# Output projection with two pairs by seven products, and the ConvFFN's first tiles reordered with six weights' low parts by accumulating transfers

## The chip, the cores and the metric

The kernel runs on one core of a Trainium2 chip. The metric is the device time of one execution in microseconds. The core has a matrix engine (PE, with weight loads shown as PEld), a vector engine (DVE), a scalar engine (ACT), a general engine (POOL) and a queue engine (SP) that issues transfers; each runs its own list of instructions in order and waits on the others through semaphores. Transfers are issued by SP, POOL and ACT, and carried out by 16 DMA engines.

## The reference

One layer of a decoder with 512 prompt tokens and 8 × 8 sample tokens, 576 columns in all, in float32, model width 1024, ConvFFN width 2816:

```python
h = _rmsnorm(x, norm1_g) * (1.0 + sc1) + sh1
...                                   # short convolution branch -> ya, attention branch -> o
yb = o @ w_attn_out
mixed = jax.nn.sigmoid(ga) * ya + jax.nn.sigmoid(gb) * yb
x = x + g1 * (mixed @ w_mix_out)

h2 = _rmsnorm(x, norm2_g) * (1.0 + sc2) + sh2
a, val = jnp.split(h2 @ w_up, 2, axis=-1)
ac, new_ffn = _causal_conv(a, ffn_buf, ffn_conv_w)
x = x + g2 * ((jax.nn.gelu(ac, approximate=False) * val) @ w_down)
```

`sh1, sc1, g1, sh2, sc2, g2` come from `silu(c) @ w_ada + b_ada`, for 9 conditioning rows (one prompt, eight samples).

## The kernel before

**Numbers in two parts.** Everything is held transposed: a tile is 128 channels by 576 tokens. Each float32 operand of a matmul is split into a high part (ACT copies it into the type float32r) and a low part (DVE subtracts the high part from the value). A product of one 128-wide output takes the 8 blocks of 128 input channels in turn (`kstep`), each as three passes, high × high, high weight × low operand, low weight × high operand, and each pass as two matmuls of 256 and 320 columns: 48 matmuls (`product`). `product_g` does one of the two column groups alone.

**Weights.** `load_w` issues a 512 KB load of 1024 × 128 weights from SP into one of four `raw` buffers; `split_w` makes `whi` (ACT) and `wlo` (DVE), each with five buffers, `split_w_slots` makes them in halves of 512 (`wh`, `wl`) in the common pool of 57 slots. A `raw` buffer comes free when its last reader is done.

**Pairs by seven products.** In other stages of the kernel two outputs are made together by a Strassen-like scheme with 7 block products instead of 8. `PairOperands` prepares the two channel blocks kp and kp + 4 of the operand: four sums of 288 columns each (DVE), high parts `th`, `nh` (ACT), low parts `tl`, `nl` (DVE), and the block called n3. `pair_weights` prepares the sums of two raw weights in steps named sums1, sums2 (DVE additions), ah, bh, ch, dh (ACT) and al, bl, cl, dl (DVE). `pair_product` then runs parts 1 to 7 of 12 matmuls with 288 columns each and combines the banks of PSUM between them: after part 1 and 3 ACT copies a bank (`p`), after part 2 and 6 DVE subtracts (`uv`), after 4, 6 and 7 the outputs are handed out (out_a0, then out_b0 and out_b1, then out_a1). A dictionary of steps says what other work is issued behind each part.

**Order around the change.** PE, ACT and DVE are pinned to the order of the program text through most of the kernel (`pinned`, class `InOrder`); elsewhere a planner that simulates a timeline orders each engine's list. The stages in question, with the times of the profile of before:

- About 473.5 to 535, the attention output (`w_attn_out`): eight whole products m = 0 to 7. DVE multiplies each result by the gate (`sg<-mm,sg`) and adds `ya`, then the sum is split into `mxh`, `mxl` (`mixed`). A generator (`filler`) puts matmuls of the second modulation block (`side_by_side`, 128 x 512, loaded as `ada` tiles of 256 KB from SP) and the transposes of its rows between the k steps, 11 steps of it to 60 ticks. The pinning ends at m = 3.
- To 588, the output projection (`w_mix_out`): first the 22 small transposes of the ConvFFN state (`state_in`), then five whole products m = 0 to 4, then the outputs 5 to 7 by halves (`mix_late`), first group 0 of all three, then group 1. After each, `residual` updates x (DVE, `x<-mm,modT,x`), ACT squares it and DVE adds the squares into `acc`. The x before the layer comes back from DRAM in two 1152 KB loads on POOL's queue (`x1`).
- Within the group 1 halves: `norm2_rows(0)` sums the squares on PE after k = `NORM2[0]` of output 5, DVE and POOL (a power of −0.5) make the row factors, and `spread_group` spreads them on PE after k = `NORM2[1]` of output 6.
- To 608.4, the first tiles of the ConvFFN: weights a0, v0 and a1 (`ws`; gate columns 0, value columns 0, gate columns 1) side by side, one k step each, while DVE, ACT and POOL make the normalised operand `h2`.
- To 640, the products v1, a2, v2, a3, v3, one after the other. A gate tile goes through pads (ACT), three taps (ACT, then DVE twice), gelu (ACT); then `value` multiplies it with its value product (`cy`, DVE) and ACT and DVE split the result (`fh`, `fl`). Between these the `PairOperands` of `h2` and the weights of the first pair are made.
- From 640 on, `FfnPair` 4 and later, by seven products each.

Of the kernel before, what the change touches and what calls it, by code (L numbers as in the profile page):

```python
# [69 lines left out]
def step_kernel(ctx: ExitStack, tc: tile.TileContext, ins: dict, outs: list):  # L70
# [30 lines left out]
    class InOrder:  # L101


        def __init__(self, engine):
            self.engine = engine
# [5 lines left out]

            return call

    pe, act, dve, pool = (InOrder(e) for e in (nc.tensor, nc.scalar, nc.vector, nc.gpsimd))
    pinned += [pe, act, dve, pool]
    matmul, transpose = pe.matmul, pe.transpose

# [27 lines left out]
    def load_w(src, nk):  # L145

        raw = wp.tile([P, nk, P], F32, tag="raw", name=nm("raw"), bufs=W_BUFS)
        nc.sync.dma_start(raw, src)
        return raw

    def split_w(raw):
        nk = raw.shape[1]
        hi = wp.tile([P, nk, P], F32R, tag="whi", name=nm("whi"), bufs=S_BUFS)
        lo = wp.tile([P, nk, P], F32R, tag="wlo", name=nm("wlo"), bufs=S_BUFS)
        split(hi, lo, raw)
        return (lambda k: hi[:, k, :]), (lambda k: lo[:, k, :])

    def split_w_slots(raw):

# [43 lines left out]
    def halves(ps):  # L203
        return ps[:, 256:512], ps[:, 512:832]

    def product(w, xs):
        ps = mmps()
        for k in range(len(xs)):
            kstep(halves(ps), w, xs, k)
            tick()  # L210
        return pf(ps)
# [17 lines left out]
    class PairOperands:  # L229

        def __init__(self, x, kp, made, values=None):
            self.x, self.kp = (x[kp], x[kp + 4]), kp
            self.r = values and (values[kp], values[kp + 4])
            self.made = made

        def sums(self):
            if not self.r:
# [11 lines left out]
        def high(self):  # L251
            made, (h0, l0), (h1, l1) = self.made, *self.x
            self.th, self.tl = slot("th", F32R), slot("tl", F32R)
            act.activation(self.th, self.t, AF.Copy)
            if self.kp % 2 == 0:
                made["n4"] = slot("nh", F32R), slot("nl", F32R)
            a, b = slice(0, HT), slice(HT, NT)
            at = (a, b)[self.kp % 2]
            nh, nl = made["n4"]
            self.nh, self.nl = nh[:, at], nl[:, at]  # L260
            act.activation(self.nh, self.r[0][:, a], AF.Copy)
            for name, hi, lo, c in (
                ("x00", h0, l0, a), ("n3", h0, l0, b), ("x10", h1, l1, a), ("x11", h1, l1, b),
                ("n1", self.th, self.tl, a), ("t2", self.th, self.tl, b), ("n4", nh, nl, at),
            ):
                made.setdefault("op", {}).setdefault(name, []).append((hi[:, c], lo[:, c]))

        def low(self):
            for lo, src, hi in ((self.tl, self.t, self.th), (self.nl, self.r[0][:, :HT], self.nh)):
                dve.tensor_tensor(out=lo, in0=src, in1=hi.bitcast(F32), op=ALU.subtract)  # L270

        def n3(self):

            (hi, lo), b = self.x[0], slice(HT, NT)
            split(hi[:, b], lo[:, b], self.r[0][:, b])

        def all(self):
            self.sums()
# [105 lines left out]
    def load(dst, src):  # L384
        return tc.keep_in_program_order(nc.sync.dma_start(dst, src))  # L385
# [315 lines left out]
    def state_load(src, n):  # L701
        parts = []
        for m0 in range(0, n, 4):
            c = min(4, n - m0)
            s = slot("st", shape=[P, 512])
            load(s[:16, : c * P], src.rearrange("o b r c -> (o b r) c")[:, m0 * P : (m0 + c) * P])
            parts.append(s)
        return parts

# [413 lines left out]
    def modulation(c0):  # L1123
# [4 lines left out]
        def rows(k):  # L1128
            cols[k] = [slot("ada", shape=[P, 512]) for _ in range(4)]
            for j, t in enumerate(cols[k]):  # L1130
                c = c0 + 512 * j
                nc.sync.dma_start(t, ins["w_ada"][0, k * P : k * P + P, c : c + 512])

        rows(0)
        yield False
# [140 lines left out]
    for n in range(len(gate_cols)):  # L1276
# [6 lines left out]
                steps[7] = lambda m=2 * n - 7: gated(m)  # L1283
        else:
            w_next[0] = weights(kpm(wao, 0), NK)
            raw = load_w(kpm(wao, P), NK)
# [40 lines left out]

    def squares(xt, m, c0=0, c1=NT):
        if m == 0:
            nc.scalar.activation(acc[:, c0:c1], xt[:, c0:c1], AF.Square)  # L1330
        else:
            sq = slot("sq")
            nc.scalar.activation(sq[:, c0:c1], xt[:, c0:c1], AF.Square)
            nc.vector.tensor_tensor(
                out=acc[:, c0:c1], in0=acc[:, c0:c1], in1=sq[:, c0:c1], op=ALU.add
            )

    stF = state_in(state_load(ins["state_ffn_conv"], NF), "stF", NF)
    A2 = cp.tile([P, NK, 9], F32, tag="A2", name="A2")
    affine(A2, 32, 56, NK)  # L1340
    x1t = [wp.tile([P, 4, NT], F32, tag="oh", name=nm("x1"), bufs=2) for _ in range(2)]
    for x in range(2):
        nc.gpsimd.dma_start(x1t[x], xT_dram[x])
    x1 = [x1t[k // 4][:, k % 4, :] for k in range(NK)]
    late = []
    for m in range(NK - 3):
        w = weights(kpm(ins["w_mix_out"][0], m * P), NK)
        if m >= NK - 6:
            late.append(split_w_slots(load_w(kpm(ins["w_mix_out"][0], (m + 3) * P), NK)))
        residual(product(w, mixed), x1[m], 16 + m)  # L1350
        squares(x1[m], m)

    def mix_late(m, g, between=None):
        ps = product_g(late[m - NK + 3], mixed, g, between=between)
        residual(ps, x1[m], 16 + m, *GRP[g])
        squares(x1[m], m, *GRP[g])

# [51 lines left out]

    for m in range(NK - 3, NK):  # L1410
        mix_late(m, 0)
    pinned.append(pe)
    mix_late(NK - 3, 1, (NORM2[0], lambda: norm2_rows(0)))
    R = {}
    ahead = []
# [8 lines left out]
    mix_late(NK - 2, 1, (NORM2[1], first_parts))  # L1424
    mix_late(NK - 1, 1)


    w_up, w_dn = ins["w_up"][0], ins["w_down"][0]

    def ffn_conv(ps, m):  # L1430
        u = padded()
# [154 lines left out]
        return load_w(kpm(w_dn, m * P, m0, m1 - m0), m1 - m0)  # L1586


    ws = [weights(kpm(w_up, c * P), NK) for c in (0, NF, 1)]
    acc2 = [mmps() for _ in range(2)]  # L1590
    first = [halves(x) for x in acc2] + [None]
    pend = [(0, k) for k in range(NK)] + [(1, k) for k in (0, 4, 1, 5, 2, 6, 3, 7)]
    for at, (g, k) in enumerate(pend):
# [12 lines left out]
            norm2_rows(1)  # L1606
        if at == NORM2[4]:
            R[1] = spread_group(r2, 1)
            pinned.extend([dve, act])
        if at == NK:  # L1610
            w_v1 = split_w_slots(load_w(kpm(w_up, FF + P), NK))
        if at == NK + 4:
# [9 lines left out]
    def w_split(raw):  # L1622
        hi, lo = (wp.tile([P, NK, P], F32R, tag=t, name=nm(t), bufs=S_BUFS) for t in ("whi", "wlo"))
        act.activation(hi, raw, AF.Copy)
        low = lambda: dve.tensor_tensor(out=lo, in0=raw, in1=hi.bitcast(F32), op=ALU.subtract)
        return ((lambda k: hi[:, k, :]), (lambda k: lo[:, k, :])), low

    def start(t, ps):
        t.copies(ps)
        t.first_tap()  # L1630
# [15 lines left out]
    tiles[0].low()  # L1646
    tiles[1].taps()
    for g, k in pend[-1 - NORM2[2] :]:
        norm2_whole(g, k)
    ops[0].high()  # L1650
    tiles[1].gelu()
    w_a3, low = w_split(raw[1])
    raw = load_w(kpm(w_up, FF + 3 * P), NK)
    pair = FfnPair(4)
    ops[0].low()
    ops[1].sums()
    value(tiles[1], v1)
    low()
    ops[1].high()
    a2 = product(w_a2, h2)  # L1660
    tiles[1].low()
    ops[1].low()
    ops[2].sums()
    v2 = product(w_v2, h2)
    start(tiles[2], a2)
    ops[2].high()
    tiles[2].taps()
    w_v3, low = w_split(raw)
    tiles[2].gelu()
    low()  # L1670
    ops[2].low()
    steps = pair.prepare()
    nxt = FfnPair(5)
    ops[3].sums()
    ops[3].high()
    steps["ah"]()
    a3 = product(w_a3, h2)
    value(tiles[2], v2)
    tiles[2].low()
    ops[3].low()  # L1680
    steps["sums1"]()
    steps["al"]()
    steps["dh"]()
    steps["bh"]()
    steps["dl"]()
    v3 = product(w_v3, h2)
    start(tiles[3], a3)
    steps["sums2"]()
    tiles[3].taps()
    tiles[3].gelu()  # L1690
    steps["ch"]()
    steps["bl"]()
    steps["cl"]()
    value(tiles[3], v3)
    tiles[3].low()

# [158 lines left out]
```

## Time and profile before

| | us |
|---|---|
| median of 3 runs | 1000.4 |
| lowest and highest run | 1000.04, 1001.07 |
| profiled execution | 1001.41 |
| its span | 999.6 |
| PE busy | 983.2 (98%) |
| DVE busy | 670.7 (67%) |
| ACT busy | 450.8 (45%) |
| POOL busy | 100.3 (10%) |

The profile is one execution with every instruction's start and duration. A line of the table by groups gives the source line, engine, operation, output<-inputs, shapes and count, then busy time and mean ns of one, then idle time before it and what ended that. A timeline row gives start and duration in us. Nearly every instruction has line 109, that of the helper `InOrder`, so groups are told apart by tile names. In the table by stretches each engine's busy time is followed by its count of instructions, then the granted clock of PE, the share of the 16 DMA engines and GB/s. Matmuls overlap in the pipeline: a duration of 0.30 us stands for a step of about 0.13 us to the next.

### The profile page before, as it was taken

How to read it: one execution, taken by the hardware profiler on the slowest of the kernel's cores; microseconds unless marked ns; L12 is line 12 of the kernel's file. 1: busy time of each engine (PE TensorE's matmuls, PEld its weight loads, DVE VectorE, ACT ScalarE, POOL GpSimd, SP SyncE). 2: the span in 40 equal slices, each digit the busy share in tenths (PEclk: the TensorE clock that was granted, in tenths of full speed). 3: DMA queues.
4: the chain of work that ended last, by engine and by line, in shares of the span. 5: the costliest groups of instructions: out<-in, count | busy, mean ns of one | idle time of the engine just before them, and what ended most of it. 6: DMA issues, size and time to landing. Idle time of an engine off the chain costs nothing.

```text
span 999.6 us, 18691 instructions
## 1 busy us (share of the span) xinstructions
PE 983.2 (98%) x7516; PEld 941.8 (94%) x7516; DVE 670.7 (67%) x1241; ACT 450.8 (45%) x835; POOL 100.3 (10%) x271
## 2 busy tenths in 40 slices
PE   7999999999999999999999999999999999999997
PEld 5899999999999989999889999999999999999997
DVE  5736676676463348788454568896569995579953
ACT  5454555545334225545232347554225552235453
POOL 2221101020000000000000021011001110001120
PEclk9999999999999999999999999999999999999999
DMA  9984332233421752235972302223233222323302
GB/s 290 319 253 109 86 90 70 86 116 115 141 76 53 246 180 85 86 106 157 338 231 72 106 11 75 65 85 106 85 101 90 85 85 86 106 65 101 110 10 95
DMA packets 173481, 119.18 MB, mean 119 GB/s; under 512 B 6887, under 2 KB 160846, under 8 KB 173106
## 3 DMA queue, kind: packets, MB, share of 16 engines
q1 hardware_dynamic: 169954, 107.00, 35.3%
q0 software_dynamic: 3296, 10.73, 3.5%
q8 instruction: 59, 0.97, 0.4%
q14 instruction: 28, 0.23, 0.1%
q10 hardware_dynamic: 144, 0.26, 0.1%
HBM read 109.17 MB, written 7.35 MB: 117 GB/s over the span
## 4 chain that ended last, share of the span: by engine, by line
PE 82%; DVE 10%; issue 2%; DMA 2%; ACT 2%; SPq 0%; POOL 0%; POOLq 0%; DVEq 0%; ACTq 0%
PE mm L109 60%; PE aux L109 19%; DVE wlo L109 3%; PE aux L1116 2%; DMA ad<-in_w_ada 2%; PE aux L1016 2%; DVE raw L109 1%; DVE uv L109 1%; DVE y L109 1%; DVE cy L109 1%; DMA raw<-in_w_in 1%; DVE fl L109 1%; SPq L385 0%; DVE wl L109 0%; ACT whi L109 0%
## 5 line engine op out<-in xcount | busy, mean ns | idle before, releaser
L109 ACT ACTIVATE whi<-raw 128x1024 fp32r<-128x1024 f32 (+2 forms) x164 | 168.1, 1034 | 178.6 <-PE mm L109 95.5
L109 DVE TENSOR_TENSOR wlo<-raw,whi 128x1024 fp32r<-128x1024 f32 (+2 forms) x164 | 195.1, 1194 | 48.6 <-ACT whi L109 47.9
L109 PE MATMUL mm<-hh,whi 128*128 128x256 f32 (+2 forms) x560 | 124.6, 299 | 0.6 <-ACT hh L109 0.6
L109 PE MATMUL mm<-hh,wlo 128*128 128x256 f32 (+2 forms) x560 | 121.8, 294 | 0.0
L109 PE MATMUL mm<-hl,whi 128*128 128x256 f32 (+2 forms) x560 | 121.0, 295 | 0.1
L109 PEld LDWEIGHTS mm<-hh,whi 128*128 128x128 f32 x560 | 93.0, 188 | 2.9 <-ACT hh L109 1.2
L109 PEld LDWEIGHTS mm<-hh,wlo 128*128 128x128 f32 x560 | 94.2, 188 | 0.0
L109 PEld LDWEIGHTS mm<-hl,whi 128*128 128x128 f32 x560 | 93.6, 188 | 0.5 <-DVE hl L109 0.5
L109 DVE SCALAR_TENSOR_TENSOR x<-mm,modT,x 128x512 f32<-128x512 f32 (+1 forms) x33 | 22.6, 686 | 71.1 <-PE mm L109 71.0
L109 PE MATMUL mm<-fh,whi 128*128 128x256 f32 (+1 forms) x304 | 65.0, 296 | 0.3 <-DVE rt L109 0.3
L109 PE MATMUL mm<-fl,whi 128*128 128x256 f32 (+1 forms) x304 | 65.1, 295 | 0.0
L109 PE MATMUL mm<-fh,wlo 128*128 128x256 f32 (+1 forms) x304 | 64.9, 295 | 0.0
L109 PE MATMUL mm<-th,whi 128*128 128x288 f32 x208 | 61.7, 297 | 0.7 <-DVE uv L109 0.7
L109 PE MATMUL mm<-th,wlo 128*128 128x288 f32 x208 | 61.6, 296 | 0.6 <-DVE wlo L109 0.6
L109 PE MATMUL mm<-tl,whi 128*128 128x288 f32 x208 | 61.4, 295 | 0.0
L109 PEld LDWEIGHTS mm<-fh,whi 128*128 128x128 f32 x304 | 50.7, 188 | 0.5 <-PE mm L109 0.5
L109 PEld LDWEIGHTS mm<-fl,whi 128*128 128x128 f32 x304 | 51.0, 188 | 0.0
L109 PEld LDWEIGHTS mm<-fh,wlo 128*128 128x128 f32 x304 | 50.8, 188 | 0.0
L867 ACT ACTIVATE s<-s,nmx 128x256 f32<-128x256 f32 (+1 forms) x72 | 34.0, 474 | 32.0 <-DVE nmx L864 31.2
L109 PE MATMUL aux<-2h,whi 128*128 128x288 f32 (+2 forms) x160 | 47.2, 295 | 0.8 <-ACT p L109 0.8
L109 PE MATMUL aux<-2h,wlo 128*128 128x288 f32 (+2 forms) x160 | 47.3, 296 | 0.0
L109 PE MATMUL aux<-2l,whi 128*128 128x288 f32 (+2 forms) x160 | 47.0, 294 | 0.0
(310 smaller groups left out, 2568.8 us busy)
## 6 DMA issues: line engine op xcount, KB each, us to landing
raw<-in_w_in SPq DMA_DIRECT2D x52, 512.0 KB, 4.2
raw<-in_w_up SPq DMA_DIRECT2D x44, 512.0 KB, 3.9
ada<-in_w_ada SPq DMA_DIRECT2D x64, 256.0 KB, 6.0
ad<-in_w_ada SPq DMA_DIRECT2D x32, 256.0 KB, 6.3
raw<-in_w_down SPq DMA_DIRECT2D x16, 512.0 KB, 3.5
raw<-in_w_conv_out SPq DMA_DIRECT2D x8, 512.0 KB, 3.5
raw<-in_w_attn_out SPq DMA_DIRECT2D x8, 512.0 KB, 4.2
raw<-in_w_mix_out SPq DMA_DIRECT2D x8, 512.0 KB, 6.1
```

The lines of the kernel that those rows point to most:

```text
L109: done = getattr(self.engine, name)(*args, **kwargs)
L867: nc.scalar.activation(s[x // 2][:, x % 2, :w], s[x // 2][:, x % 2, :w], AF.Exp, bias=nmx[:, x : x + 1], accum_out=den[:, x : x + 1],)
L1016: done = nc.tensor.matmul(O[HALF[par], :256], vt(i - nkt + 1 + kt)[:, hd * 64 : hd * 64 + 64], pts[kt][:, par * 256 : par * 256 + 256], st ...
L1116: done = nc.tensor.matmul(ps[32 * j : 32 * j + 32, :], cT[:, k, :], cols[k][j], start=(k == 1), stop=(k == NK - 2),)
```

## The change

- **Two pairs in the output projection.** `w_mix_out`'s outputs 1 and 2, and 3 and 4, are made by `pair_product`; output 0 and the halves of 5 to 7 stay. The operands of the pairs are made between the attention output products, whose order becomes 0, 4, 1, 5, 2, 6, 3, 7 so that blocks kp and kp + 4 are there together; the weights of the first pair are prepared there as well (`PAIR_LOW`, `PAIR_HIGH`). `PairOperands` gets a form (`beside`) that keeps the n3 block apart, since the unchanged block of `mixed` is still needed by the later products.
- **Loads and order there.** The attention output weights are loaded and split up to three products ahead. DVE, ACT and PE stay pinned throughout, and SP is pinned too from here on, with the modulation, state and weight loads in program order. The filler's rate becomes 11/44. The two loads of x1 and those of the ConvFFN state go to SP, behind the weight load of the seventh product.
- **Squares and late weights** are issued as steps of the pairs and halves. `NORM2[0]` becomes 5.
- **Low parts by accumulating transfers.** For six weights (a0, v0, a1 of the first tiles, and v2, a3, v3) ACT writes the high part, then the negated raw weight into `wlo`, and POOL issues a 512 KB transfer that adds `raw` to it: the sum of the negated copy, rounded to float32r, and the raw value is the low part. `raw` comes free when the transfer has landed.
- **First tiles of the ConvFFN.** Tiles 0 and 1 go side by side through pads, taps and gelu, and the work beside v1 to v3 is shifted: operands and pair weights are made earlier, tile 3 starts ahead of v3's product.

```diff
-NORM2 = 4, 0, 3, 1, 3
+NORM2 = 5, 0, 3, 1, 3
+PAIR_LOW = {2: "sums1", 3: "al", 4: "dl", 5: "sums2", 6: "bl"}
+PAIR_HIGH = {2: "ah", 3: "dh", 5: "bh", 6: "ch"}
...
+    def w_split_adding(raw):
+        hi, lo = (wp.tile([P, NK, P], F32R, tag=t, name=nm(t), bufs=S_BUFS) for t in ("whi", "wlo"))
+        act.activation(hi, raw, AF.Copy)
+
+        def low():
+            act.activation(lo, raw, AF.Copy, scale=-1.0)
+            pool.dma_start(lo, raw, accum_op=ALU.add)
+
+        return ((lambda k: hi[:, k, :]), (lambda k: lo[:, k, :])), low
...
-    filler[1] = 11 / 60
-    mixed = []
-    for m in range(NK):
-        if m + 1 < NK and m + 1 not in w_next:
-            w_next[m + 1] = weights(kpm(wao, (m + 1) * P), NK)
-        ps = product(w_next.pop(m), o)
-        if m == 3:
-            pinned.clear()
-        t = gb[m]
+    pinned.append(sync)
+    filler[1] = 11 / 44
+    w_mix = ins["w_mix_out"][0]
+    mixed, values, made_mix = [None] * NK, [None] * NK, {}
+    ops, steps = [], {}
+    order = [m for kp in range(4) for m in (kp, kp + 4)]
+
+    def mixed_in(m, ps, between):
+        values[m] = t = gb[m]
         dve.tensor_tensor(out=t, in0=ps, in1=t, op=ALU.mult)
         dve.tensor_tensor(out=t, in0=t, in1=ya[m], op=ALU.add)
-        mixed.append(split_slot(t, "mx"))
+        mixed[m] = hi, lo = slot("mxh", F32R), slot("mxl", F32R)
+        act.activation(hi, t, AF.Copy)
+        for step in between:
+            step()
+        dve.tensor_tensor(out=lo, in0=t, in1=hi.bitcast(F32), op=ALU.subtract)
+
+    def w_high(i):
+        src = kpm(wao, order[i] * P) if i < NK else kpm(w_mix, 0)
+        w_next[i], lows[i] = w_split(load_w(src, NK))
+
+    lows = {}
+    w_high(2)
+    for i, m in enumerate(order):
+        ps = product(w_next.pop(i), o)
+        if i + 2 in lows:
+            lows.pop(i + 2)()
+        if i == 1:
+            raws = [load_w(kpm(w_mix, c * P), NK) for c in (1, 2)]
+            w_pair, steps = pair_weights(*raws)
+            del raws
+        between = [steps[n] for n in PAIR_LOW.get(i, "").split()]
+        if i and i % 2 == 0:
+            between.append(op.low)
+        mixed_in(m, ps, between)
+        if i + 3 <= NK:
+            w_high(i + 3)
+        for n in PAIR_HIGH.get(i, "").split():
+            steps[n]()
+        if i % 2:
+            op = PairOperands(mixed, i // 2, made_mix, values, beside=True)
+            op.sums()
+            op.high()
+        if i == 4:
+            ffn_state = state_load(ins["state_ffn_conv"], NF)
+            x1t = [wp.tile([P, 4, NT], F32, tag="oh", name=nm("x1"), bufs=2) for _ in range(2)]
+            for x in range(2):
+                sync.dma_start(x1t[x], xT_dram[x])
+    op.low()
+    steps["cl"]()
     drain()
...
+    ps = product(w_next.pop(NK), mixed, order)
+    stF = state_in(ffn_state, "stF", NF)
     affine(A2, 32, 56, NK)
-    for m in range(NK - 3):
-        w = weights(kpm(ins["w_mix_out"][0], m * P), NK)
-        if m >= NK - 6:
-            late.append(split_w_slots(load_w(kpm(ins["w_mix_out"][0], (m + 3) * P), NK)))
-        residual(product(w, mixed), x1[m], 16 + m)
-        squares(x1[m], m)
+    residual(ps, x1[0], 16)
+    w_pair2, steps = pair_weights(*raws)
+    steps = in_turn(steps)
+    steps[5] = lambda: squares(x1[0], 0)
+    steps[6] = lambda: late_weights(5)
+    mix_pair(w_pair, 1, 2, steps)
+    steps = {
+        1: lambda: squares(x1[1], 1), 2: lambda: late_weights(6), 3: lambda: squares(x1[2], 2),
+        4: lambda: late_weights(7), 5: lambda: ws.append(first_w()),
+    }
+    mix_pair(w_pair2, 3, 4, steps)
...
-    start(tiles[0], pf(acc2[0]))
+    tiles[0].copies(pf(acc2[0]))
+    tiles[1].copies(first[2])
     ops[0].sums()
-    tiles[0].taps()
-    w_v2, low = w_split(raw[0])
-    tiles[0].gelu()
+    for t in tiles[:2]:
+        t.first_tap()
+    for t in tiles[:2]:
+        t.taps()
+    w_v2, low = w_split_adding(raw[0])
+    for t in tiles[:2]:
+        t.gelu()
     low()
     v1 = product(w_v1, h2)
     value(tiles[0], pf(acc2[1]))
-    start(tiles[1], first[2])
+    value(tiles[1], v1)
...
     a2 = product(w_a2, h2)
...
+    w_v3, low = w_split_adding(raw)
     low()
...
+    v2 = product(w_v2, h2)
...
+    a3 = product(w_a3, h2)
+    start(tiles[3], a3)
+    steps["ch"]()
+    tiles[3].taps()
+    steps["cl"]()
+    tiles[3].gelu()
     v3 = product(w_v3, h2)
-    start(tiles[3], a3)
```

More of the change, by code (lines that the diff above doesn't have):

```diff
@@ L112, in __getattr__ @@
             return call
[L114 removed]
+    pe, act, dve, pool, sync = (
+        InOrder(e) for e in (nc.tensor, nc.scalar, nc.vector, nc.gpsimd, nc.sync)
+    )
     pinned += [pe, act, dve, pool]
@@ L204, in halves, with product @@
         return ps[:, 256:512], ps[:, 512:832]
-    def product(w, xs):
+    def product(w, xs, order=None):
         ps = mmps()
-        for k in range(len(xs)):
+        for k in order or range(len(xs)):
             kstep(halves(ps), w, xs, k)
@@ L1336, in squares @@
             )
[L1338 removed]
     A2 = cp.tile([P, NK, 9], F32, tag="A2", name="A2")
[L1340 to L1351 removed]
+    x1 = [x1t[k // 4][:, k % 4, :] for k in range(NK)]
@@ L1620, in step_kernel @@
     ops = [PairOperands(h2, kp, made2, h2_raw) for kp in range(4)]
[L1622 to L1626, printed above, removed]
     def start(t, ps):
@@ L1644, in step_kernel @@
     value(tiles[0], pf(acc2[1]))
-    start(tiles[1], first[2])
-    tiles[0].low()
-    tiles[1].taps()
+    value(tiles[1], v1)
+    ops[1].sums()
+    for t in tiles[:2]:
+        t.low()
+    ops[0].high()
     for g, k in pend[-1 - NORM2[2] :]:
         norm2_whole(g, k)
-    ops[0].high()
-    tiles[1].gelu()
-    w_a3, low = w_split(raw[1])
+    w_a3, low = w_split_adding(raw[1])
+    low()
     raw = load_w(kpm(w_up, FF + 3 * P), NK)
@@ L1655, in step_kernel @@
     ops[0].low()
-    ops[1].sums()
-    value(tiles[1], v1)
-    low()
     ops[1].high()
+    ops[2].sums()
     a2 = product(w_a2, h2)
-    tiles[1].low()
     ops[1].low()
-    ops[2].sums()
-    v2 = product(w_v2, h2)
     start(tiles[2], a2)
```

93 lines of the change are left out of this document (61 added, 32 removed).

## The prediction

> **What bounds the kernel now.** I read the page first (busy shares, clock, the chain that ended last), then the table by stretches for the part that changes, then the timelines of DVE, PE and ACT there, for when each product ends.
>
> ```profile
> span 999.6 us, 18691 instructions
> PE 983.2 (98%) x7516; PEld 941.8 (94%) x7516; DVE 670.7 (67%) x1241; ACT 450.8 (45%) x835; POOL 100.3 (10%) x271
> PE 82%; DVE 10%; issue 2%; DMA 2%; ACT 2%; SPq 0%; POOL 0%; POOLq 0%; DVEq 0%; ACTq 0%
> ```
> ```profile
> core 0: us, PE busy (x) PEld busy (x) DVE busy (x) ACT busy (x) POOL busy (x), PEclk, DMA share, GB/s
> 475.00:495.00 20.00, 19.66 (x148) 16.00 (x147) 9.73 (x13) 5.43 (x8) 0.99 (x2) 1.00 1.03 387
> ...
> 445.00:500.00 55.00, 54.66 (x411) 51.00 (x411) 36.53 (x52) 22.16 (x36) 1.10 (x2) 1.00 0.68 235
> 500.00:545.00 45.00, 45.00 (x342) 40.41 (x341) 23.53 (x30) 14.15 (x18) 0.00 (x0) 1.00 0.52 157
> 545.00:560.00 15.00, 15.00 (x116) 15.00 (x115) 8.24 (x15) 5.58 (x8) 0.00 (x0) 1.00 0.43 123
> 560.00:590.00 30.00, 30.00 (x231) 29.86 (x230) 15.76 (x39) 7.22 (x16) 2.92 (x9) 1.00 0.16 45
> 608.00:640.00 32.00, 32.00 (x244) 32.00 (x243) 27.90 (x47) 21.16 (x37) 3.90 (x14) 1.00 0.17 50
> ```
>
> PE is busy 98% of the span, at the full granted clock (PEclk 1.00) in every stretch that changes. So time is saved by taking matmuls away, or by closing the few gaps of PE; work taken from DVE is worth nothing by itself. The profiled execution took 1001.41 us (span 999.6 and 1.8 around it), 1.0 above the median of 1000.4; I add up against 1001.4 and subtract 1.0 at the end. A run of this kernel can be told from no change by about 0.2%, 2 us.
>
> How fast PE goes is read from when DVE takes each product's result:
>
> ```profile
> 479.95 0.76 DVE L109 TENSOR_TENSOR sg<-mm,sg 128x576 f32<-128x576 f32 x1 [1.14 <-PE mm L109]
> 488.36 0.76 DVE L109 TENSOR_TENSOR sg<-mm,sg 128x576 f32<-128x576 f32 x1 [3.87 <-PE mm L109]
> 534.28 0.76 DVE L109 TENSOR_TENSOR sg<-mm,sg 128x576 f32<-128x576 f32 x1 [3.00 <-PE mm L109]
> 548.91 0.75 DVE L109 SCALAR_TENSOR_TENSOR x<-mm,modT,x 128x512 f32<-128x512 f32 x1 [3.52 <-PE mm L109]
> 555.25 0.75 DVE L109 SCALAR_TENSOR_TENSOR x<-mm,modT,x 128x512 f32<-128x512 f32 x1 [0.90 <-PE mm L109]
> 567.93 0.75 DVE L109 SCALAR_TENSOR_TENSOR x<-mm,modT,x 128x512 f32<-128x512 f32 x1 [2.49 <-PE mm L109]
> 640.09 0.30 PE L109 MATMUL aux<-2h,whi 128*128 128x288 f32 x1
> 640.23 0.30 PE L109 MATMUL aux<-2l,whi 128*128 128x288 f32 x1
> ```
>
> A whole product is 6.34 us (555.25 − 548.91): 48 matmuls of 288 columns in the mean, 0.132 each. The 288-column ones of a pair start 0.13–0.14 apart. A product with a full group of modulation matmuls takes 8.41 (488.36 − 479.95), so a group is 2.07.
>
> **The change, part by part.**
>
> *1. Four whole products become two pairs.* 192 matmuls become 2 × 7 × 12 = 168 of 288 columns: 24 × 0.132 = **−3.17 us**, all on PE. Their operands are new work of DVE and ACT, beside the eight attention output products:
>
> ```profile
> L109 DVE TENSOR_TENSOR wlo<-raw,whi 128x1024 fp32r<-128x1024 f32 x43 | 52.3, 1221 | 5.9 <-ACT whi L109 5.6
> L109 DVE TENSOR_TENSOR sg<-mm,sg 128x576 f32<-128x576 f32 x8 | 6.1, 756 | 19.8 <-PE mm L109 19.8
> L109 DVE TENSOR_TENSOR tl<-tw,th 128x576 fp32r<-128x576 f32 x4 | 3.0, 753 | 0.5 <-ACT th L109 0.5
> L109 DVE TENSOR_TENSOR tw<-t 128x288 f32<-128x288 f32 x4 | 1.8, 452 | 0.0
> L109 DVE TENSOR_TENSOR raw<-raw,raw 128x512 f32<-128x512 f32 x7 | 5.0, 719 | 0.0
> ```
>
> In the new order DVE's fullest stretch is the last three products: three gate multiplies, adds and low parts of `mixed` (9 × 0.756), two sets of four sums (8 × 0.452), two of operand lows (2 × 0.753 and 4 × 0.452), two raw sums (2 × 0.719) and three whole weight lows (3 × 1.221): 18.8 us against 19.0 of PE and the transposes of the last modulation rows. It fits barely, at no cost. If it doesn't, part 2 of the first pair waits: it needs the last weight low ("cl"), ready about 540–541 on the clock of before, used about 542.4. Part 3 of the second pair reads a bank that DVE empties behind out_b0, out_b1 and two late weight lows: ready 554.4 to 554.9, wanted 554.9. Bounds 0 and 0.5 (one more 288-column step): I take **+0.3**.
>
> *2. Modulation groups one to a product (11/60 to 11/44).* From the first to the eighth product before took 534.28 − 479.95 = 54.33. Seven products and four groups are 7 × 6.34 + 4 × 2.07 = 52.7; the other 1.67 is the rows' four transposes (some 0.5, an estimate: four steps of 0.132) and a group cut in two by its loads. In the new order each group stands whole behind the first k of products two to five, as where 8.41 was measured twice running: **−1.1**. The cover: the loads now go out in program order on SP, each behind a buffer that DVE empties. The last two are issued about 500.5 and used 505.7, with a landing of 4.4 to 6.2:
>
> ```profile
> DMA to landing us min/median/max: 4.4/6.0/6.2
> ```
>
> (the ada tile, 480 to 530). So 0 to 1.0 is lost there; I keep 0, because the two 1152 KB loads of x1, which stand on POOL's queue at 474.9 and 479.1 where the DMA share is 1.03, have moved behind them. Those two loads and the six of the state are now on SP behind the weight load of the seventh product (about 503); what queues behind them is the first `w_mix_out` weight, issued about 518 and split about 525. Nothing waits for x1 before 539, so no cost.
>
> *3. Six weights' low parts by transfers.* DVE loses 6 × 1.22, ACT gets six negated copies like this one, POOL six issues:
>
> ```profile
> L109 ACT ACTIVATE whi<-raw 128x1024 fp32r<-128x1024 f32 x45 | 46.9, 1053 | 37.2 <-PE mm L109 13.5 <-DMA raw<-in_w_up 6.2 <-issue 5.9
> L109 ACT ACT_TABLE_LOAD x1 | 1.3, 1283 | 0.0
> 579.21 0.73 POOL L109 TENSOR_TENSOR r<-r,mhalf 128x2 f32<-128x2 f32 x1 [99.56 <-DVE r L109]
> xT_dram<-xT POOLq DMA_DIRECT2D x4, 576.0 KB, 6.3
> q<-low POOLq DMA_DIRECT2D x16, 128.0 KB, 3.3
> DMA to landing us min/median/max: 3.1/7.0/9.4
> ```
>
> (the last row is the xT_dram tile, its four 576 KB and two 1152 KB transfers). Before has no accumulating transfer, so I count what each may take, from issue to first use. First tiles: ACT makes two high and two negated copies in a row (4 × 1.05) from about 572.8 to 577.0; the third weight is used at 583.5: 6.5 us. (The second waits on POOL for the 0.73 power, goes out about 575.9 and is used at 583.2.) v2: ACT is through pads, taps, table load and two gelus about 7.1 after v1 starts, used 13.1 after: 6.0. a3: 13.1 to 19.6: 6.5. v3: 20.4 to 26.0: 5.6. A delay of v2 gives a3 and v3 the same time more, since v3's copies follow a2, not v2. With a landing L the cost is max(0, L − 6.5) + max(0, L − 5.6). L is between 3.1 (best 576 KB) and 9.4 (worst): 0 to 6.7. The nearest in size is the 576 KB median, 6.3: **+0.7**.
>
> The Trainium skill, "DMA: Bandwidth & Descriptors", section "Anatomy of one DMA — SWDGE (gpsimd) path", fits such a transfer as 2.0 us plus bytes over 436 GB/s: 3.2 for 512 KB, an estimate by which this term would be 0 and the time 0.7 lower. The trace disagrees: 3.35 by that fit for 576 KB, where the row has 6.3.
>
> *4. First tiles side by side, NORM2[0] 4 to 5.* The gaps that end here are those of before at its first FFN pair:
>
> ```profile
> 641.44 1.22 DVE L109 TENSOR_TENSOR wlo<-raw,whi 128x1024 fp32r<-128x1024 f32 x1 [0.58 <-ACT whi L109]
> 642.59 0.81 DVE L109 TENSOR_TENSOR cy<-mm,y 128x512 f32<-128x512 f32 x2
> 642.72 0.40 PE L109 MATMUL mm<-th,wlo 128*128 128x288 f32 x1 [0.62 <-DVE wlo L109]
> 645.36 1.04 ACT L109 ACTIVATE whi<-raw 128x1024 fp32r<-128x1024 f32 x1
> 646.31 0.38 ACT L109 COPY p<-aux 128x288 f32<-128x288 f32 x1
> 646.74 0.40 PE L109 MATMUL aux<-2h,whi 128*128 128x288 f32 x1 [0.84 <-ACT p L109]
> ```
>
> The pair's weight low is late (0.62), so DVE takes the value of tile 3 late, so ACT makes its high and the copy p late (0.84). Afterwards a3 stands ahead of v3, and "ch", "cl" run beside v3: both gaps go, **−1.46**; late next is p, by 0 to 0.2. In exchange a2 waits until value v0 is multiplied, which now follows two sets of pads, two taps, a weight copy, the table load and gelu: 6.35 to 6.5 after v1 starts, against 6.38 of v1. And the row factors now have 9 matmuls (1.3 us) instead of 12 to hide DVE, the 0.73 on POOL and the hops. Each 0 to 0.5; together **+0.5**.
>
> **Sum.** −3.17 − 1.1 − 1.46 + 0.3 + 0.7 + 0.5 = −4.2: 1001.4 − 4.2 − 1.0 = 996.2, say **996.2 us**.
>
> **Rivals.**
> *All is hidden.* Landing below 5.6 and no new gap: −5.7, 994.7. Against: three margins of under 0.5 us.
> *The pairs are fed late (no change).* For: 18.8 of some 19.4 us on DVE, on queues pinned in order, where one late weight shifts everything behind; the modulation loads have 5.2 us for 4.4 to 6.2. Part 2's wait 1.5, the group's 1.0 and part 3's 0.5 make 3.0 in place of 0.3: 998.9.
> *Transfers land late (slower).* An accumulation must also fetch what it adds to, so L could pass the 9.4 of the rows. By the formula it costs all that the rest saves (4.9) at L = 8.5, and 2 us more at L = 9.5; at 11 it costs 9.9 instead of 0.7: 1005.4. For: DVE is 27.90 of 32 us busy while POOL issues them. The Trainium skill, "SBUF — State Buffer", section on the "DVE blocks DMA" trap, has POOL's descriptors starve while DVE runs a two-port operation, 3.1 us for 0.62. Against, by its own list: tensor_tensor, nearly all that DVE runs here, has no such mode. In before q<-low landed in 3.3 beside such work.
>
> **How the numbers follow.** Forecast 0.50, all hidden 0.14, fed late 0.16 (0.03 of it still faster by 0.2%), transfers late 0.16 (0.02 of it within 0.2%), something unnamed and slower 0.04. Faster 0.67, within 0.2% 0.15, slower 0.18. The range leaves out the far end of the late transfers and what is unnamed: 994.0 to 1002.5. The forecast's own range is 995 to 998.
>
> **What would show it.** PE rows down by 24, PE busy by about 3 us; from the first to the eighth product 53.2 instead of 54.33; the pairs' results some 4.5 us earlier than x<-mm at 567.93; no wlo or p wait at the first FFN pair; accumulating transfers of 512 KB landing in 4 to 7 us. Wrong if PE waits for "DMA wlo" above 2 us in all, if PE waits for DVE between the eighth product and the late halves above 1 us, or if a new wait of a2 for cy is above 1 us.

## The result, and the profile after

The changed kernel takes **994.21 us** (median of 6 runs, 993.77 to 995.13) against 1000.40 (6 runs, 1000.04 to 1001.46): a ratio of 0.9937, with a 95% interval of 0.9927 to 0.9948. That is 6.2 us less where 4.2 were forecast, inside the forecast's range, outside its narrow one (995 to 998), and nearest to the rival in which all is hidden (994.7). The profiled execution took 995.13, with a span of 993.4; it is the slowest of the six, of which two took about 995.1 and four 993.8 to 994.2.

The page of the changed kernel: span, busy times, and the chain that ended last by engine.

```profile
span 993.4 us, 18735 instructions
PE 977.9 (98%) x7492; PEld 939.1 (95%) x7492; DVE 688.8 (69%) x1289; ACT 464.6 (47%) x861; POOL 103.7 (10%) x275
PE 88%; DVE 4%; DMA 3%; issue 2%; ACT 1%; SPq 0%; POOL 0%; POOLq 0%; DVEq 0%; ACTq 0%
```

PE has 24 matmuls and 5.3 us less, and its share of the chain went from 82% to 88%: DVE, which held 10% of it, now holds 4%, although it is busier (688.8 for 670.7).

To place the gain I cut both profiles at six DVE rows, each of which takes a result of PE (the last one, the output tiles, follows it by POOL). In the kernel before (the other two cuts, 479.95 and 534.28, are rows of the prediction):

```profile
442.82 0.45 DVE L109 TENSOR_TENSOR uv<-mm,p 128x288 f32<-128x288 f32 x1
576.44 0.48 DVE L109 SCALAR_TENSOR_TENSOR x<-aux,modT,x 128x256 f32<-128x256 f32 x1 [1.44 <-PE aux L109]
648.76 0.45 DVE L109 TENSOR_TENSOR uv<-mm,p 128x288 f32<-128x288 f32 x1
993.95 1.41 DVE L109 TENSOR_SCALAR yo<-aux,r 128x512 f32<-128x512 f32 x2 [0.81 <-POOL r L109]
```

The same rows of the changed kernel's timeline:

```profile
442.12 0.45 DVE L111 TENSOR_TENSOR uv<-mm,p 128x288 f32<-128x288 f32 x1
479.26 0.76 DVE L111 TENSOR_TENSOR sg<-mm,sg 128x576 f32<-128x576 f32 x1
532.41 0.76 DVE L111 TENSOR_TENSOR sg<-mm,sg 128x576 f32<-128x576 f32 x1 [1.60 <-PE mm L111]
571.31 0.48 DVE L111 SCALAR_TENSOR_TENSOR x<-aux,modT,x 128x256 f32<-128x256 f32 x1 [1.08 <-PE aux L111]
642.20 0.45 DVE L111 TENSOR_TENSOR uv<-mm,p 128x288 f32<-128x288 f32 x1
987.29 1.41 DVE L111 TENSOR_SCALAR yo<-aux,r 128x512 f32<-128x512 f32 x2 [0.81 <-POOL r L111]
```

| stretch | before | changed | difference |
|---|---|---|---|
| gate pairs (442) to first attention output product | 37.13 | 37.14 | 0 |
| first to eighth attention output product | 54.33 | 53.15 | −1.18 |
| on to the third half of the output projection | 42.16 | 38.90 | −3.26 |
| on to the first FFN pair's first uv | 72.32 | 70.89 | −1.43 |
| on to the last output tile | 345.19 | 345.09 | −0.10 |
| from 442 to the end | 551.13 | 545.17 | −5.96 |

The 0.70 by which the changed kernel stands ahead at 442 is no part of the change, which edits nothing before: in the fourteen profiles of this study that row starts between 441.34 and 443.33. So 6.0 us is what the edits earned between these two executions, in three places.

The second row, the 1.18, is not idle time of PE. In the kernel before, one of the four groups of modulation matmuls is cut in two and slow (PE's timeline):

```profile
503.57 1.90 PE L1116 MATMUL aux<-ada,cT 128*32 128x512 f32 x10
505.86 1.06 PE L1116 MATMUL aux<-ada,cT 128*32 128x512 f32 x6
```

A whole group of sixteen takes 1.92. The two products around the cut one take 15.95 together (496.77 to 512.72), where in the changed kernel a product with a group takes 8.41 and one without 6.36, 14.77 together: that is the whole 1.18.

PE's waits in the changed kernel, and where its one new wait falls (the timelines of PE, DVE and ACT); the two short waits for uv lie outside the stages that change:

```profile
PE mm L111 <- DVE uv L111: 0.4, 2, 0.2
PE mm L111 <- DMA wlo<-raw: 0.4, 1, 0.4
```
```profile
628.95 0.44 PE L111 MATMUL mm<-2l,whi 128*128 128x256 f32 x2
629.80 0.53 PE L111 MATMUL mm<-2h,wlo 128*128 128x256 f32 x2 [0.41 <-DMA wlo<-raw]
630.17 0.43 PE L111 MATMUL mm<-2h,whi 128*128 128x256 f32 x2
636.02 0.82 DVE L111 TENSOR_TENSOR cy<-mm,y 128x512 f32<-128x512 f32 x2 [2.67 <-PE mm L111]
639.75 0.38 ACT L111 COPY p<-aux 128x288 f32<-128x288 f32 x1
```

Both waits at the first FFN pair are gone: DVE now stands idle for 2.67 until v3's product ends, and takes the value at once. In their place v3 waits for its transfer. The row says 0.41; the steps say more. 628.95 to 629.80 is 0.85 where two matmuls take 0.26, and the next step is 0.37: 0.70 lost. The same count on the two rows of before gives 0.89 (641.81 to 642.72 to 642.96) and 1.11 for waits shown as 0.62 and 0.84. So the two waits cost 2.0, the new one 0.7, and 1.3 of the 1.43 is told by them.

### The profile page after: what moved, and what is told of

The parts are those of the page before. It is cut to its first block, busy times and chain, and to the rows that moved or that the text cites. A ratio compares the mean times of both kernels' runs of the same rounds, so it can differ in the third digit from the quotient of the medians.

```text
span 993.4 us, 18735 instructions
## 1 busy us (share of the span) xinstructions
PE 977.9 (98%) x7492; PEld 939.1 (95%) x7492; DVE 688.8 (69%) x1289; ACT 464.6 (47%) x861; POOL 103.7 (10%) x275
## 4 chain that ended last, share of the span: by engine, by line
PE 88%; DVE 4%; DMA 3%; issue 2%; ACT 1%; SPq 0%; POOL 0%; POOLq 0%; DVEq 0%; ACTq 0%
PE mm L111 63%; PE aux L111 22%; PE aux L1049 2%; PE aux L1149 1%; DMA ad<-in_w_ada 1%; DVE wlo L111 1%; DMA wlo<-raw 1%; DMA raw<-in_w_in 1%; SPq L418 0%; DVE uv L111 0%; DVE raw L111 0%; DVE y L111 0%; DVE cy L111 0%; ACT whi L111 0%; DVE fl L111 0%
## 5 line engine op out<-in xcount | busy, mean ns | idle before, releaser
L111 ACT ACTIVATE whi<-raw 128x1024 fp32r<-128x1024 f32 (+2 forms) x166 | 170.2, 1034 | 150.6 <-PE mm L111 80.6
L111 DVE TENSOR_TENSOR wlo<-raw,whi 128x1024 fp32r<-128x1024 f32 (+2 forms) x160 | 190.4, 1193 | 47.3 <-ACT whi L111 46.8
L111 PE MATMUL mm<-th,whi 128*128 128x288 f32 x224 | 66.6, 297 | 0.4 <-DVE uv L111 0.4
L111 PE MATMUL mm<-th,wlo 128*128 128x288 f32 x224 | 66.1, 295 | 0.0
L111 PE MATMUL mm<-tl,whi 128*128 128x288 f32 x224 | 66.0, 295 | 0.0
L111 DVE SCALAR_TENSOR_TENSOR x<-mm,modT,x 128x512 f32<-128x512 f32 (+1 forms) x29 | 19.6, 676 | 57.7 <-PE mm L111 57.7
```

The lines of the kernel that those rows point to most:

```text
L111: done = getattr(self.engine, name)(*args, **kwargs)
```

## Experiments

Each was timed beside the kernel before on the same chip. "442 to end" and "last half to first pair" are measured in its profile by the rows above (changed kernel: 545.17 and 70.89; before: 551.13 and 72.32). Where a few tenths matter I go by these, since they leave out the start of the kernel; each is one execution, and the last stretch alone (first FFN pair to the last output tile, which no edit touches) differs by up to 0.4 between them.

| run | edit | median us | ratio to before (95%) | 442 to end | last half to first pair |
|---|---|---|---|---|---|
| e1_dve_lows | all six lows by DVE | 997.52 | 0.9966 (0.9955–0.9978) | 547.68 | 73.43 |
| e2_old_tiles | first tiles' order of before, v2, a3, v3 by DVE | 996.32 | 0.9957 (0.9942–0.9972) | 546.38 | 72.34 |
| e3_v_dve | v2, a3, v3 by DVE | 996.87 | 0.9961 (0.9947–0.9976) | 546.91 | 72.55 |
| e4_v3_dve | v3 by DVE | 995.52 | 0.9948 (0.9933–0.9963) | 545.35 | 71.07 |
| e5_whole | whole products for the pairs | 998.11 | 0.9973 (0.9962–0.9984) | 548.12 | 70.87 |
| e6_filler60 | filler 11/60 | 1000.44 | 0.9992 (0.9982–1.0001) | 549.97 | 70.67 |
| e7_plain | plain copies, the sum left out | 994.59 | 0.9937 (0.9920–0.9953) | 544.46 | 70.19 |
| e8_before44 | before, with filler 11/44 | 1000.71 | 0.9999 (0.9989–1.0008) | 550.71 | 72.26 |
| e9_x1_pool | x1's loads on POOL, early | 997.45 | 0.9972 (0.9961–0.9983) | 547.63 | 70.11 |
| e10_v3_first | v3's negated copy first | 994.18 | 0.9934 (0.9922–0.9947) | 544.53 | 70.19 |
| e11_old_tiles_adding | first tiles' order of before, lows by transfers | 996.36 | 0.9957 (0.9942–0.9973) | 546.08 | 71.91 |
| e12_norm4 | `NORM2[0]` 4 | 994.82 | 0.9942 (0.9928–0.9955) | 544.44 | 70.16 |

### The pairs alone: e5

```diff
-    mix_pair(w_pair, 1, 2, steps)
...
-    mix_pair(w_pair2, 3, 4, steps)
+    for m in range(1, NK - 3):
+        residual(product(w, mixed, order), x1[m], 16 + m)
```

with the pairs' operands and weights left out.

> The changed kernel with outputs 1 to 4 of the output projection as four whole products again, without the pairs' operands and weights; order of the attention output products, loads, transfers and first tiles as changed. Theory, 24 matmuls and nothing else: 3.2 above the changed kernel, 997.4. Rival, feeding the pairs costs PE something that now comes back: 996.4 to 996.9.

From the eighth attention output product (532.82) to the third half (574.57) it takes 41.75, the changed kernel 38.90: 2.85 for 24 matmuls. Four whole products are 4 × 6.34 = 25.36, less 2.85 is 22.51 for 168 matmuls: 0.134 a step where I had 0.132. The theory holds in this stretch; by the median its 997.4 was 0.7 too low (998.11), and e5 has a wait of 0.5 for the row factors ("POOL r") that the changed kernel has not. There is no other cost of feeding the pairs: no wait of PE stands between 538 and 566 in the changed kernel, and the second part of DVE's last combination (uv at 553.88), which I had put 0 to 0.5 late, holds nothing up. The remaining 0.41 of this stretch (42.16 − 41.75) came without the pairs; in the kernel before the 22 state transposes are in two pieces (20 at 540.64, 2 at 542.32), in the changed kernel in one. What held the last two was not tried.

### The modulation groups: e6, e8, e9

```diff
# e8, on the kernel before; e6 is the reverse on the changed kernel
-    filler[1] = 11 / 60
+    filler[1] = 11 / 44
```
```diff
# e9, on the changed kernel
-            for x in range(2):
-                sync.dma_start(x1t[x], xT_dram[x])
...
+    for x in range(2):
+        pool.dma_start(x1t[x], xT_dram[x])
     lows = {}
     w_high(2)
```

> The kernel before with the filler's rate 11/44 alone. Theory A, the rate decides: 53.2 to 53.5 from the first to the eighth attention output product instead of 54.33, 999.3. Theory B, the loads of x1 on POOL at 475 to 479 make the modulation tiles late and the rate alone gives nothing or loses: 1000.4 or more, with waits of PE for ada tiles.

> The changed kernel with x1's two 1152 KB loads on POOL's queue again, ahead of the attention output products; the state's loads and everything else as changed. Theory, the even modulation groups need these loads out of their way: a wait of PE for an ada tile of about 0.8 and 54.0 instead of 53.15 from the first to the eighth attention output product; 0.8 above the changed kernel. Rival, SP in program order issues the tiles early enough anyway: 53.15.

> The changed kernel with the filler's rate of before, 11/60 for 11/44. Theory A, the rate alone decides (a group of modulation matmuls cut by its loads and standing where its tiles are late): about 1 lost between the first and the eighth attention output product (54.2 instead of 53.15): 995.2. Theory B, the loads of x1 that went away made the tiles late: 53.15 as before, 994.2.

First to eighth product: 53.15 in the changed kernel, 54.04 in e8 (479.61 to 533.65), 56.46 in e9 (480.46 to 536.92), 58.09 in e6 (478.48 to 536.57). The waits of PE, of e8, e9 and e6 in turn:

```profile
PE aux L1116 <- DMA ada<-in_w_ada: 0.8, 1, 0.8
```
```profile
PE aux L1149 <- DMA ada<-in_w_ada: 3.2, 2, 2.5
```
```profile
PE aux L111 <- ACT row L1179: 3.4, 1, 3.4
```

In the kernel before the rate alone is worth 0.3 there, and nothing that the medians show (1000.71 for 1000.81): theory B. All four groups are whole, which gives back the 1.18, but the second comes 3.4 us earlier (489.58 for 493.03) and waits 0.8 for its tiles, beside x1's loads, so that its product takes 9.31 instead of 8.41. With x1's loads back in the changed kernel (e9) it is worse than before: 3.3 lost where the theory had 0.8. The rows put it down to SP's list in order: the next eight ada tiles go out from 490.26, behind weight loads, where the changed kernel has 482.65. No run has SP free beside these loads and all else as changed, so that is a reading. So the even groups need both parts of the edit; the cover that I named, x1's loads out of the way, was the right one, but its price was 3.3 and not the 1.0 that I put on it.

e6 is a new thing, which neither theory had: 4.9 lost in this stretch, and 5.8 by the medians beside the kernel before (its profiled execution, 999.12, is among its fastest). With the old rate the last groups fall into the fifth and sixth products, their tiles hold up SP, the `w_mix_out` weights behind them go out 3.5 later (514.99 for 511.44), and ACT in order waits 2.85 for such a weight with the copy of the modulation rows behind it:

```profile
523.67 2.00 ACT L111 ACTIVATE whi<-raw 128x1024 fp32r<-128x1024 f32 x2 [2.85 <-DMA raw<-in_w_mix_out]
526.82 0.56 ACT L1179 COPY row<-aux 128x512 f32<-128x512 f32 x1
```

PE, in order too, waits for that copy. In the kernel before, SP is not pinned and PE and ACT only up to the fourth product; that this is why the rate does little there was not tried by itself.

### Who needs the transfers: e1, e2, e3, e11

```diff
# e3 (e1: also in first_w)
-    w_v2, low = w_split_adding(raw[0])
+    w_v2, low = w_split(raw[0])
...                                     # a3, v3 likewise
# e2: the lines from "raw = [load_w(...)" to tile 3's low as in the kernel before; e11: the same with w_split_adding
```

> The changed kernel with all six low parts made by DVE again (high and low as in the other weights), the transfers and negated copies left out. Theory A, the transfers earn little and the new order earns the end of the two waits: 994.2 to 995.2; v3's wait of 0.41 for its transfer goes, a2 waits some 0.3 to 0.5 for cy because v2's low part (1.22) stands ahead of it on DVE, and the first weights' lows put the row factors off by up to 0.7. Theory B, DVE was what held the first tiles and the transfers freed it: 996 or more, with waits of PE for DVE (cy, wlo, uv) above 1.5 us between 602 and 650.

> The changed kernel with the order of before in the products v1 to v3 and their lows (v2, a3, v3) by DVE as before; the pairs, loads and the first three weights' transfers stay. Theory: the waits of the first FFN pair for wlo (0.62) and p (0.84) come back and cost 1.4 to 1.8: 995.6 to 996.0. Rival, the gain after 608 is not from the order: 994.2 with no such waits.

> The changed kernel with the lows of v2, a3 and v3 by DVE in the new order; the first three weights keep their transfers. Theory A: 993.7 to 994.6, v3's wait for its transfer gone, a wait of a2 for cy of 0.3 to 0.5 in its place. Theory B, DVE has no room there: 995.4 or more, the waits of the first FFN pair back.

> The order of before in the products v1 to v3, but v2, a3 and v3 by accumulating transfers; the rest as changed. From the gate pairs at 442 to the end, old order with DVE's lows took 546.4, new order with DVE's lows 546.9, new order with transfers 545.2. Theory A, order and transfers need each other: 546.0 or more, the old order gains little from transfers since ACT, now longer, is what its value of tile 3 waits for. Theory B, the transfers alone earn it: 545.2 or less.

In e1 and e3 my theory A fell. e3 is theory B's, in time and in the wait for p (0.8). e1 has theory B's time, but not its waits: PE waits for DVE only 0.4, and longer for ACT's p (0.9) and for the row factors (0.6). In e2 the theory held for the waits, 0.5 for wlo and 0.8 for p, and e11 has theory A's 546.1. Last half to first pair:

| | lows of v2, a3, v3 by DVE | by transfers |
|---|---|---|
| order of before | 72.34 (e2) | 71.91 (e11) |
| new order | 72.55 (e3) | 70.89 (changed), 70.19 without v3's wait (e10) |

By itself the new order gains nothing (72.55 for 72.34), and the transfers by themselves 0.43; together they gain 1.45, or 2.15. The medians, each beside its kernel before, say the same of the pair and less of the 0.43: e2 gains 4.3, e3 3.75, e11 4.2, the changed kernel 6.2. e3 shows why, in its timelines of DVE, ACT and PE:

```profile
623.11 1.23 DVE L111 TENSOR_TENSOR wlo<-raw,whi 128x1024 fp32r<-128x1024 f32 x1 [1.72 <-ACT whi L111]
637.65 0.81 DVE L111 TENSOR_TENSOR cy<-mm,y 128x512 f32<-128x512 f32 x2
641.38 0.37 ACT L111 COPY p<-aux 128x288 f32<-128x288 f32 x1
641.80 0.40 PE L111 MATMUL aux<-2h,whi 128*128 128x288 f32 x1 [0.82 <-ACT p L111]
```

v3's low stands in DVE's list behind ACT's high part, which stands behind a gelu: DVE does nothing for 1.72, and all behind it is up to 1.72 + 1.23 later. From there to 637.65 DVE has no gap. So tile 3's value at 637.65 waits for DVE's own list (no idle time before it), p is late and PE waits 0.82, as before the change. In the changed kernel the same wait stands on POOL's queue, where nothing is behind it, and DVE goes on to the sums and the pair's weights. That is what the transfer buys by these rows: for v3, 1.72 of waiting and 1.23 of busy time. No run takes away the one without the other. In e11 DVE has the lows off its list, but in the order of before the pair's last low (with 0.58 of waiting for ACT) stands between v3's product and its value, and the wait for p stays:

```profile
636.23 1.23 DVE L111 TENSOR_TENSOR wlo<-raw,whi 128x1024 fp32r<-128x1024 f32 x1 [0.58 <-ACT whi L111]
637.37 0.82 DVE L111 TENSOR_TENSOR cy<-mm,y 128x512 f32<-128x512 f32 x2
```

The first three weights' transfers are worth 0.77 (547.68 − 546.91, e1 against e3): without them PE has a wait of 0.6 for the row factors ("POOL r"), as I had feared for the shorter cover. It stands in e5 too, with 0.5.

### What a transfer costs: e7, e4, e10

```diff
# e7
-            pool.dma_start(lo, raw, accum_op=ALU.add)
+            pool.dma_start(lo, raw)
# e10, for v3 alone
+        act.activation(lo, raw, AF.Copy, scale=-1.0)
         act.activation(hi, raw, AF.Copy)
-            act.activation(lo, raw, AF.Copy, scale=-1.0)
```

e4 is the edit of e3 for v3 alone.

> The changed kernel with the six accumulating transfers as plain copies of the same bytes from the same queue (so the low parts hold the raw weights: the sum is left out). Theory A, the accumulation has a price of its own, since it also fetches what it adds to: landing 3.5 to 4.5 instead of 4.7 to 7.1, v3's wait gone, 993.7. Theory B, the landing is that of any such transfer from POOL: 5 to 6.5, 994.2.

> The changed kernel with only v3's low by DVE. Theory: PE's wait for the transfer (0.41, about 0.55 with the refilling of the pipeline) goes and nothing takes its place: 993.6. Rival: value of tile 2 and the pair's steps behind it on DVE are late by 1.2 and a wait of the first FFN pair takes its place: 994.2 or more.

> The changed kernel with v3's negated copy ahead of its high part on ACT, so that its transfer goes out 0.95 earlier. Theory: v3's wait of 0.41 goes and no wait of the first FFN pair takes its place, as with plain copies (there 0.7 less from the gate pairs at 442 to the end than in the changed kernel): 993.5 to 993.8. Rival, as with v3's low by DVE, the wait for p takes its place: 994.2.

The wlo tile on POOL's queue: first its row in the list of transfers, then issue to landing in us (min, median, max), of the changed kernel and of e7.

```profile
wlo<-raw POOLq DMA_DIRECT2D x6, 512.0 KB, 5.9
...
DMA to landing us min/median/max: 4.7/5.9/7.1
```
```profile
wlo<-raw POOLq DMA_DIRECT2D x6, 512.0 KB, 3.4
...
DMA to landing us min/median/max: 2.8/3.4/5.0
```

In these two profiles the accumulation costs 2.5 us beyond a plain copy of the same bytes: theory A of e7, but for its time (994.59 for 993.7). The 2.5 is no constant: six other profiles with the six accumulating transfers (e5, e6, e9 to e12) have medians of 4.5 to 5.7, 1.1 to 2.3 above the one profile of plain copies. v3's transfer was issued at 623.18 and landed at 629.76: 6.6, which is the 0.4 too much. Without its wait the kernel is 0.70 shorter between last half and first pair, in e7 and in e10 alike: 70.19 in both. With v3's low by DVE instead (e4) PE waits 0.4 for p, and nothing is gained: the rival. By the stretch e4 is 0.9 longer than e10.

e10 has no such wait in its profile, as its theory has it, yet its median, 994.18, is that of the changed kernel and not below 993.8, and e7's is no lower. e5, e9 and e12 have no such wait either, with v3's list untouched: there v3's transfer landed in 4.4, 5.3 and 5.8, while e6, with 6.1, waits 0.3. So the wait comes and goes between executions. That most runs of the changed kernel are without it would explain the equal medians, and its profiled execution is the slowest of the six; the other five have no trace kept, so it is not shown.

### NORM2 alone: e12

```diff
-NORM2 = 5, 0, 3, 1, 3
+NORM2 = 4, 0, 3, 1, 3
```

> The changed kernel with NORM2[0] at 4 as before: the rows' sums one k step earlier, 12 matmuls between them and the spread instead of 9. Theory A, the squares are summed later now, so the rows wait for DVE: a wait of PE for DVE acc of 0.2 to 0.6, 0.2 to 0.6 above the changed kernel. Theory B, it makes no difference: same within 0.2 on the trace.

Theory B: 70.16 is e10's 70.19, the other profile without v3's wait, and PE waits neither for acc nor for the row factors at either setting. So this part of the change earned nothing that these profiles show.

## Why the prediction was right, and where it was off

The forecast had the right three places and a gain of 4.2 where 6.0 to 6.2 was measured. By the sum of the prediction:

| step | forecast | measured | by |
|---|---|---|---|
| 24 matmuls | −3.17 | −2.85 | e5; a step of a pair takes 0.134 |
| feeding the pairs | +0.3 | 0 | no wait of PE in the pairs |
| modulation groups | −1.1 | −1.18 | rows of both kernels |
| waits at the first FFN pair | −1.46 | −2.0 | steps around the waits |
| v3's transfer | +0.7 | +0.7, in the profiled execution | e7 and e10, 70.89 to 70.19 |
| cy for a2, row factors | +0.5 | 0 | no such waits |
| state transposes and unplaced | 0 | −0.6 | remainder of −5.96 |

**Sizes.** The first two rows are right only together, −2.87 for −2.85: the 0.3 put down to feeding lies in the step of a pair, 0.134 for 0.132. The +0.5 was taken from bounds though the rows left room. Tile 0's value (cy) ran at 608.28 and was done at 609.10, 5.9 after v1's first matmul (603.24) where I had 6.35 to 6.5; a2 began at 609.61, so 0.5 was to spare. And the two waits were priced by the idle time that a row shows, 1.46, instead of by the steps around them, 2.0.

**The step that was wrong.** "Work taken from DVE is worth nothing by itself" was read off PE's busy share, so the sum has the transfers as a cost alone (+0.7), and part 4 put the whole end of the two waits down to the new order. e3 and e11 show that neither order nor transfers do it alone: with the new order and the lows on DVE the wait for p is 0.8 again and nothing is gained, and in that order the transfers are worth 1.66 (72.55 to 70.89). The chain of the kernel before, cut to 608 to 646, says otherwise (its shares by engine and line):

```profile
by line: DVE wlo L109 12.4%; ACT whi L109 10.0%; ACT y L109 7.9%; DVE tl L109 7.7%; DVE tw L109 6.6%; DVE y L109 6.3%; DVE cy L109 6.1%; issue 5.9%; DVE raw L109 5.3%; ACT fh L109 5.1%; DVE t L109 4.7%; ACT t L109 4.2%; DVE nl L109 3.9%; AC
```

What ended last there was a zigzag of DVE and ACT, with wlo as its largest piece and no PE among the large ones, though PE was busy nearly all the time. The prediction argues from the whole span alone, where PE's 82% of the chain hides this. In the changed kernel the same view, from 603 to 640, begins with PE:

```profile
by line: PE mm L111 40.6%; DMA wlo<-raw 17.8%; PE aux L111 5.5%; ACT whi L111 5.2%; ACT wlo L111 5.1%; DVE y L111 4.6%; ACT t L111 4.3%; ACT y L111 4.1%; ACT th L111 3.1%; issue 2.4%; DVE cy L111 2.2%; ACT fh L111 1.9%; ACT nh L111 1.8%; AC
```

What is left of DVE, ACT and the transfer there is the way to v3's wait. In e12, which has no such wait, the same view, from 603 to 640, is PE alone:

```profile
by line: PE mm L111 94.2%; PE aux L111 6.1%
```

**The transfer's price.** The +0.7 came out by luck. I took 6.3 from a 576 KB transfer to DRAM, and the measured median is 5.9; but that is two errors that cancel, a plain transfer put too high and the accumulation left out. v3's had about 6.0 to land in and not 5.6 (623.18 to 629.21, two steps of 0.13 behind 628.95), it took 6.6, and three of the four other profiles with its list untouched (e5, e9, e12) have no such wait at all. The estimate from the Trainium skill's "DMA: Bandwidth & Descriptors", section "Anatomy of one DMA — SWDGE (gpsimd) path", 3.2 for 512 KB, which I had set aside, is close to the plain copy of e7 (3.4). What neither gave is the price of accumulating, 2.5 in the changed kernel's profile. The starving of POOL's descriptors beside DVE that "SBUF — State Buffer" of the Trainium skill describes does not show here: e7's copies landed in 2.8 to 5.0 beside the same DVE work, nearly all tensor_tensor and scalar_tensor_tensor.

**The rivals.** "Late transfers" needed 8.5 us to eat the gain; the worst was 7.1. Of "The pairs are fed late" only the part on the modulation groups came true, and only in e6 and e9, where one edit of the set is taken back; the pairs themselves are not late there either (38.78 and 38.74 from the eighth product to the third half, for 38.90). "All is hidden" has the right time, with v3's wait not hidden and a larger gain from the old waits.

## What to carry to other kernels

Price a wait by the steps around it, not by the idle time in its row: here 0.41, 0.62 and 0.84 cost 0.70, 0.89 and 1.11. When work is moved off an engine, look at what that work waits for: v3's low took 1.23 of DVE, and the wait in front of it, in a long in-order list, another 1.72; on POOL's queue nothing stood behind that wait. Read the chain stage by stage, since its share of the whole span can hide the stage that another engine bounds. And an edit of order, loads and rates on pinned queues is one edit: in their stretch, taking back the rate alone cost 4.9 us, x1's loads alone 3.3, though in the kernel before the rate was worth 0.3 there.

## What the runs showed of the hardware

An accumulating transfer of 512 KB from SBUF to SBUF landed in 5.9 us (the median of six in the changed kernel's profile; 4.5 to 5.7 in six other profiles), a plain one in 3.4 (e7); on POOL its issue took 0.90 against 0.57.

A wait of PE of 3.4 us costs more than itself. In e6, the table by stretches around the wait for the rows' copy (PE, PEld, DVE, ACT, POOL busy; then the granted clock, the DMA share and GB/s):

```profile
518.00:523.80 5.80, 5.80 (x46) 5.79 (x44) 5.04 (x9) 0.82 (x2) 0.00 (x0) 1.00 1.03 378
523.80:527.40 3.60, 0.23 (x2) 0.00 (x0) 0.00 (x0) 3.58 (x6) 0.00 (x0) 0.92 0.23 69
527.40:528.40 1.00, 0.97 (x5) 0.97 (x6) 0.00 (x0) 0.00 (x0) 0.00 (x0) 0.50 0.00 0
528.40:529.40 1.00, 1.00 (x6) 1.00 (x6) 0.81 (x2) 0.00 (x0) 0.00 (x0) 0.50 0.06 16
529.40:530.40 1.00, 1.00 (x7) 1.00 (x6) 1.00 (x2) 0.00 (x0) 0.00 (x0) 0.57 0.00 0
530.40:531.40 1.00, 1.00 (x10) 1.00 (x9) 0.96 (x2) 0.00 (x0) 0.00 (x0) 1.00 0.21 61
```

Within the wait, the same table in smaller steps:

```profile
526.70:526.80 0.10, 0.00 (x0) 0.00 (x0) 0.00 (x0) 0.10 (x1) 0.00 (x0) 1.00 0.00 0
526.80:526.90 0.10, 0.00 (x0) 0.00 (x0) 0.00 (x0) 0.10 (x2) 0.00 (x0) 0.77 0.00 0
526.90:527.00 0.10, 0.00 (x0) 0.00 (x0) 0.00 (x0) 0.10 (x2) 0.00 (x0) 0.50 0.00 0
```

The granted clock fell to half some 2.8 us after PE's last matmul had ended (524.0 as the profile models it), and came back at 530.3, about 2.8 after PE went on at 527.43. That costs another 1.4, an estimate: half of 2.8. It fits the loss, 4.94 in the stretch for a wait of 3.41. In e9 a wait of 2.49 (498.77 to 501.26) left the clock at 1.00. The Trainium skill, "TensorE: Matmul & The Clock Gate", section "What's actually happening", gives an idle window of about 3.4 us for this. e9 agrees with it, and the clock stayed low for 3.4 (526.9 to 530.3); in e6 it fell sooner than 3.4 after the last matmul.
